# The first block of the first FFN: both token halves on the first half of the inputs, partial sums kept in SBUF, then the second half of the inputs

## Chip, cores and metric

The kernel runs on one core of a Trainium2 chip. The metric is device time in microseconds (us) of one execution, the median of the runs shown. The engines are TensorE (PE; its weight loads are PEld), VectorE (DVE), ScalarE (ACT), GpSimd (POOL) and SyncE (SP), which issues most of the DMAs.

## What is computed

One step of a hybrid decoder layer over 1024 prompt tokens and 32 sample tokens. The change lies at the very start, in the first of two SwiGLU FFNs (D_MODEL 1024, D_FF 2816):

```python
def swiglu(h, w_gate, w_up, w_down):
    return (jax.nn.silu(h @ w_gate) * (h @ w_up)) @ w_down

def modulated(h, g, i):
    return rms_norm(h, g) * (1 + scale[:, i]) + shift[:, i]

mod = (jax.nn.silu(c) @ p['w_ada'] + p['b_ada'])
x = x + 0.5 * gate[:, 0] * swiglu(modulated(x, p['g_ffn1'], 0), p['w1_gate'], p['w1_up'], p['w1_down'])
...
```

Attention, a gated MLP mixer and a second FFN of the same shape follow; the change does not touch them.

## The kernel before, in words

**Arithmetic.** Inputs are fp32. Each operand is split into a rounded part `hi` and a remainder `lo`, both fp32r, and `mm3` (L324, L325, L326) makes one product of three matmuls: hi·hi, hi·lo, lo·hi. A `hi` is a cast on ACT (L186 and L330 for weights, L741 for inputs), a `lo` a subtraction on DVE (L187, L331, L745).

**Blocks.** D_FF is cut into 11 blocks of 256. In each block, inputs (1024 in 2 halves of 512, each of 4 tiles j) and tokens (1024 in 2 halves of 512) make a 2 by 2 problem for the gate weights ("g") and the up weights ("u"). Blocks 1 to 10 do it in seven products instead of eight, on sums of weights (`sums_s` on POOL, L256 to L259) and on sums T1 to T4 of the inputs. Block 0 does it plainly in four stages, since the sums of the inputs don't exist yet. A stage is named (token half, input half). Its inputs are B11 for (0,0), B21 for (0,1), B12 for (1,0) and B22 for (1,1). In a stage each of g and u has two groups f of 12 matmuls, so a stage has 48. A group accumulates in one PSUM bank `psa`; there are four.

**Order before.** Block 0 runs (0,0), (0,1), (1,0), (1,1). A bank filled in (0,0) stays open and (0,1) adds to it; then `fin` empties it: for g a silu on ACT from PSUM (L862), for u a multiply on DVE with the silu (L864). The other branch of `fin`, used in later blocks, first adds a kept partial sum u: for g a DVE add (L860) and a silu from SBUF (L862), for u a DVE add into `hf` (L867) and a multiply on POOL (L868).

**Work between.** Fillers are generators whose steps are put into the program after every six matmuls (`tick`), at a pace given when they are added. The instructions of every engine then run in the order in which they were recorded; an engine stops at an instruction that waits. `mid1` adds and finishes the fillers at the stage bounds:
- `second` and `f1a`: norm and transposes of token half 1 (L525, L531, L553), giving B12 (ACT L755 and L741, DVE L745).
- ahead of (0,1), in one piece: the conditioning of quarters 2 and 3 of the inputs: `ada_q` (PE L362, ACT L365), `ada_m` (PE L374, DVE L377 to L379), `x_mod` (DVE L387, ACT L741, DVE L745), giving B21.
- `f1b`: the rest of the transposes, giving B22; then T1, T2 and T3 (`T23`), T4. One step of T1 or T2 is a subtraction on DVE (L775), a cast on ACT (L741), and the `lo` on DVE (L745). The subtractions of T3 and T4 are on POOL (L775); their casts and `lo`s are as the others.
- `s_norm` and `sample_gu`: the sample tokens (PE L404, L593, L610, L622, L628; DVE L407, L602, L603, L612, L642, L630, L650).

Block 1 begins with matmuls on the weights `ws`, whose `lo` (DVE L331) stands on DVE behind all of T1 to T4.

## Time and profile before

| | |
|---|---|
| median of 3 runs | 2425.75 us (2423.23 to 2427.13) |
| the profiled execution | 2428.47 us, span 2426.5 us |
| busy share of the span: PE, DVE, POOL, ACT | 96%, 56%, 36%, 34% |
| block 0, from its first matmul to the first one of block 1 | 29.43 to 108.22 us |

The profile is one execution. PE is busy almost throughout, but less so at the start: the first two of the 40 slices of the span show 6 and 8 tenths for PE, most others 9. So the stretch from 29 to 110 us is read by itself, stage by stage, with the work of each engine in order of time and what ended each idle stretch. A busy matmul runs into the next one: a group's pitch is the distance of starts, not the duration that a row names.

### The profile page before, as it was taken

How to read it: one execution, taken by the hardware profiler on the slowest of the kernel's cores; microseconds unless marked ns; L12 is line 12 of the kernel's file. 1: busy time of each engine (PE TensorE's matmuls, PEld its weight loads, DVE VectorE, ACT ScalarE, POOL GpSimd, SP SyncE). 2: the span in 40 equal slices, each digit the busy share in tenths (PEclk: the TensorE clock that was granted, in tenths of full speed). 3: DMA queues.
4: the chain of work that ended last, by engine and by line, in shares of the span. 5: the costliest groups of instructions: out<-in, count | busy, mean ns of one | idle time of the engine just before them, and what ended most of it. 6: DMA issues, size and time to landing. Idle time of an engine off the chain costs nothing.

```text
span 2426.5 us, 37080 instructions
## 1 busy us (share of the span) xinstructions
PE 2328.4 (96%) x12977; PEld 1738.7 (72%) x12977; DVE 1363.3 (56%) x1922; ACT 823.2 (34%) x1413; POOL 869.0 (36%) x822
## 2 busy tenths in 40 slices
PE   6899999999998999999999999999799999999998
PEld 4677777776776775556677767776577777777876
DVE  4756566564457555664443454445566565656557
ACT  4322222323234244543332242233332223233433
POOL 1455656550024123243323220011156565552125
PEclk8999999999999999999999999999899999999999
DMA  6243444459755237567877634443144434357743
GB/s 260 83 152 127 157 143 141 150 189 403 281 199 199 89 97 214 166 178 235 234 197 229 217 118 132 163 139 109 49 158 145 147 131 158 133 173 300 254 157 136
DMA packets 192784, 421.13 MB, mean 174 GB/s; under 512 B 22003, under 2 KB 80308, under 8 KB 192598
## 3 DMA queue, kind: packets, MB, share of 16 engines
q1 hardware_dynamic: 179510, 382.06, 46.7%
q0 software_dynamic: 12800, 36.19, 5.5%
q8 instruction: 102, 1.67, 0.3%
q14 instruction: 84, 0.69, 0.1%
q10 hardware_dynamic: 288, 0.52, 0.1%
HBM read 338.36 MB, written 78.23 MB: 172 GB/s over the span
## 4 chain that ended last, share of the span: by engine, by line
PE 78%; issue 5%; DVE 5%; DMA 5%; ACT 2%; POOL 2%; POOLq 1%; SPq 1%; DVEq 0%; ACTq 0%
PE psa L324 16%; PE psa L325 15%; PE psa L326 15%; PE psb L324 7%; PE psb L325 7%; PE psb L326 7%; PE pss L622 2%; DVE wlo L187 2%; PE psa L441 1%; PE pss L1587 1%; POOLq L1544 1%; DMA pk<-in_kvp 1%; PE pss L683 1%; DMA nat<-in_kvn 1%; PE pss L1633 1%
## 5 line engine op out<-in xcount | busy, mean ns | idle before, releaser
L187 DVE TENSOR_TENSOR wlo<-w,whi 128x1024 fp32r<-128x1024 f32 (+1 forms) x273 | 306.0, 1163 | 177.6 <-ACT whi L186 177.1
L324 PE MATMUL psa<-xT,ws 128*128 128x512 f32 x800 | 317.7, 397 | 0.0
L326 PE MATMUL psa<-xT,ws 128*128 128x512 f32 x800 | 311.9, 390 | 2.0 <-DVE ws L331 2.0
L325 PE MATMUL psa<-xT,ws 128*128 128x512 f32 x800 | 312.4, 391 | 0.0
L186 ACT CAST whi<-w 128x1024 fp32r<-128x1024 f32 (+1 forms) x273 | 241.2, 927 | 138.6 <-PE psb L325 35.9
L324 PEld LDWEIGHTS psa<-xT,ws 128*128 128x128 f32 x800 | 150.1, 188 | 45.7 <-ACT h L862 8.2
L326 PEld LDWEIGHTS psa<-xT,ws 128*128 128x128 f32 x800 | 150.2, 188 | 34.9 <-DVE ws L331 2.8
L325 PEld LDWEIGHTS psa<-xT,ws 128*128 128x128 f32 x800 | 150.2, 188 | 29.5
L868 POOL TENSOR_TENSOR h<-hf,h 128x512 f32<-128x512 f32 x60 | 93.1, 1552 | 218.0 <-DVE hf L867 180.9
L331 DVE TENSOR_TENSOR ws<-wsum,ws 128x512 fp32r<-128x512 f32 x160 | 153.0, 956 | 24.1 <-ACT ws L330 24.1
L324 PE MATMUL psa<-xT,whi 128*128 128x512 f32 x384 | 161.7, 421 | 1.6 <-ACT xT L741 1.6
L325 PE MATMUL psa<-xT,whi 128*128 128x512 f32 x384 | 153.6, 400 | 0.0
L326 PE MATMUL psa<-xT,wlo 128*128 128x512 f32 x384 | 153.0, 399 | 0.0
L331 DVE TENSOR_TENSOR ws<-w,ws 128x512 fp32r<-128x512 f32 x120 | 120.0, 1000 | 50.5 <-ACT ws L330 50.5
L324 PE MATMUL psa<-whi 128*128 128x512 f32 x308 | 124.9, 405 | 6.3 <-ACT whi L186 6.3
L325 PE MATMUL psa<-wlo,whi 128*128 128x512 f32 x308 | 121.8, 396 | 7.5 <-DVE wlo L187 7.5
L324 PE MATMUL psb<-xT,ws 128*128 128x512 f32 x320 | 127.1, 397 | 0.0
L325 PE MATMUL psb<-xT,ws 128*128 128x512 f32 x320 | 125.1, 391 | 0.0
L324 PE MATMUL psb<-whi 128*128 128x512 f32 x308 | 124.8, 405 | 0.0
L326 PE MATMUL psb<-xT,ws 128*128 128x512 f32 x320 | 124.6, 389 | 0.0
L326 PE MATMUL psa<-whi,wlo 128*128 128x512 f32 x308 | 121.4, 394 | 0.0
L1545 POOL DMA_DIRECT2D nat<-in_kvn x128 | 70.9, 554 | 140.4 <-issue 54.1
(397 smaller groups left out, 4898.4 us busy)
## 6 DMA issues: line engine op xcount, KB each, us to landing
wada<-in_w_ada SPq DMA_DIRECT2D x72, 512.0 KB, 7.1
x<-x SPq DMA_DIRECT2D x40, 512.0 KB, 5.6
pk<-in_kvp SPq DMA_DIRECT2D x128, 144.0 KB, 3.4
pk<-in_kvp POOLq DMA_DIRECT2D x128, 144.0 KB, 3.6
w<-w1h SPq DMA_DIRECT2D x35, 512.0 KB, 6.8
w<-w2h SPq DMA_DIRECT2D x35, 512.0 KB, 7.0
nat<-in_kvn SPq DMA_DIRECT2D x128, 128.0 KB, 2.9
nat<-in_kvn POOLq DMA_DIRECT2D x128, 128.0 KB, 3.0
```

The source lines that it names most:

```text
L186: self.nc.scalar.copy(hv(w.hi), src)
L187: self.nc.vector.tensor_tensor(out=hv(w.lo), in0=src, in1=hv(w.hi), op=ALU.subtract)
L324: nc.tensor.matmul(out, sh, mh, start=first, stop=False, skip_group_check=cont)
L325: nc.tensor.matmul(out, sh, ml, start=False, stop=False, skip_group_check=cont)
L326: nc.tensor.matmul(out, sl, mh, start=False, stop=last, skip_group_check=cont)
L331: self.nc.vector.tensor_tensor(out=lo, in0=src, in1=hi, op=ALU.subtract)
L441: nc.tensor.matmul(ps[32 * k:32 * k + 32, 256 * qq:256 * qq + 256], self.sc[:, 4 * kh + k, :], t[:, k, :], start=(kh == 0), stop=(kh == 1))
L622: self.nc.tensor.matmul(ps[32 * j:32 * j + 32, cols], st[:, k, :], mv, start=(k < 4), stop=(k >= nk - 4))
L683: self.nc.tensor.matmul(ps[32 * j:32 * j + 32, 0:256], hT[:, f, :], r[f][:, j // 2, c], start=(f == 0), stop=(f == 1))
L868: nc.gpsimd.tensor_tensor(out=g, in0=t, in1=g, op=ALU.mult)
L1544: v = eng.value_load(self.pt[0:1, 32 * b + i:32 * b + i + 1], min_val=0, max_val=self.a[name].shape[0] - 1)
L1545: eng.dma_start(out=out, in_=self.a[name][bass.ds(v, 1)].rearrange(pat))
```

## The change

`plan_ffn` gets a switch, on for the first FFN and off for the second. With it block 0 runs (0,0), (1,0), (0,1), (1,1). Each of the eight groups of the first two stages is closed and copied by ACT from PSUM to SBUF (`uv`); the groups of the last two stages open a new bank, and `fin` gets the copy as its u. In `mid1` the conditioning of quarters 2 and 3 becomes a filler in (1,0), f1b, T1 and `s_norm` stay in (0,1), and T2, T3, T4 and `sample_gu` share (1,1).

```diff
+        plan["conv"] = ((0, 0, "g"), (1, 0, "u"), (0, 1, "g")) if turns else ((0, 0, "g"), (0, 0, "u"), (0, 1, "g"))
+        plan["order"] = [(0, 0), (1, 0), (0, 1), (1, 1)] if turns else [(0, 0), (0, 1), (1, 0), (1, 1)]
...
-                for half in range(2):
-                    for kh in range(2):
+                for i, (half, kh) in enumerate(plan["order"]):
...
-                                if not kh:
+                                held = (half, f, n) in part
+                                if not kh or held:
                                     T[n, f] = self.psa()
...
                                 if kh:
-                                    fin(n, "%d%d" % (f + 1, half + 1), None, T[n, f])
+                                    fin(n, "%d%d" % (f + 1, half + 1), part.get((half, f, n)), T[n, f])
+                                elif plan["turns"]:
+                                    if not f:
+                                        uv = self.u([P, 2, 512], F32, name="uv")
+                                    part[half, f, n] = uv[:, f]
+                                    nc.scalar.copy(uv[:, f], T[n, f])
...
-        plan1 = k.plan_ffn("w1")
+        plan1 = k.plan_ffn("w1", True)
-        plan2 = k.plan_ffn("w2")
+        plan2 = k.plan_ffn("w2", False)
...
             if stage == (0, 0):
                 k.f1 = k.add(second(), 1.6)
+            elif stage == (1, 0):
+                k.f1.finish()
+
+                def quarters():
+                    for q in (2, 3):
+                        k.ada_q(q, k.psb)
+                        yield
+                    for q in (2, 3):
+                        k.ada_m(q)
+                    for q in (2, 3):
+                        k.x_mod(X1, f01, q)
+                        yield
+
+                k.f1 = k.add(quarters(), 1.5, 4.5)
             elif stage == (0, 1):
                 k.f1.finish()
-                for q in (2, 3):
-                    k.ada_q(q, k.psb)
-                for q in (2, 3):
-                    k.ada_m(q)
-                for q in (2, 3):
-                    k.x_mod(X1, f01, q)
                 k.f1 = k.add(chain(f1b, T1), 1.1)
                 k.f2 = k.add(k.s_norm(0, k.ada_rows()), 0.95)
-            elif stage == (1, 0):
-                k.f1.finish()
-                k.f2.finish()
-                k.f1 = k.add(T23, 1.2)
-                k.f2 = k.add(sample_gu(plan1["b"][0]), 1.2)
             elif stage == (1, 1):
                 k.f1.finish()
                 k.f2.finish()
-                k.f1 = k.add(T4, 1.3)
+                k.f1 = k.add(chain(T23, T4), 0.85)
+                k.f2 = k.add(sample_gu(plan1["b"][0]), 1.2)
             elif stage == (2, 0):
                 k.f1.finish()
+                k.f2.finish()
```

The lines of `mm3` and behind it stand three lower in the changed kernel (L326 is L329 there, L331 is L334, L642 is L645, L745 is L748, L775 is L778, L860 is L863, L862 is L865, L867 is L870, L868 is L871). The order in which instructions stand shows at three places what moves; `hf` is the sum of a kept and a new partial sum, `xt` is T2, `wsum` the weight sums of block 1.

PE, from the end of the second stage's matmuls or from within them. Before, the end of (0,0), the conditioning, the start of (0,1):

```order
L326 MATMUL psa<-xT,wlo 128x512
L362 MATMUL psb<-wada,sc 32x256 x32
L374 MATMUL pss<-cst,g_196 128x1 x8
L324 MATMUL psa<-xT,whi 128x512
L325 MATMUL psa<-xT,whi 128x512
```

Changed, within (1,0), from the second `ada_q` on:

```order
L365 MATMUL psb<-wada,sc 32x256 x16
L327 MATMUL psa<-xT,whi 128x512
L328 MATMUL psa<-xT,whi 128x512
L329 MATMUL psa<-xT,wlo 128x512
L327 MATMUL psa<-xT,whi 128x512
L328 MATMUL psa<-xT,whi 128x512
L329 MATMUL psa<-xT,wlo 128x512
L377 MATMUL pss<-cst,g_196 128x1 x8
```

The conditioning has moved behind 30 to 42 matmuls of (1,0), and six more follow it before (0,1) begins.

DVE, from the second step of T1 to the first copy of the sample's G. Before:

```order
L775 TENSOR_TENSOR xf<-xf 128x512
L745 TENSOR_TENSOR xT<-xf,xT 128x512
L864 TENSOR_TENSOR h<-h,psa 128x512
L775 TENSOR_TENSOR xf<-xf 128x512
L745 TENSOR_TENSOR xT<-xf,xT 128x512
L612 COPY xsT<-pss 128x2x4x32
L775 TENSOR_TENSOR xf<-xf 128x512
L745 TENSOR_TENSOR xT<-xf,xT 128x512
L864 TENSOR_TENSOR h<-h,psa 128x512
L775 TENSOR_TENSOR xt<-xf 128x512
L745 TENSOR_TENSOR xT<-xt,xT 128x512
L642 COPY G<-pss 128x256
```

Changed:

```order
L778 TENSOR_TENSOR xf<-xf 128x512
L748 TENSOR_TENSOR xT<-xf,xT 128x512
L870 TENSOR_TENSOR hf<-uv,psa 128x512
L778 TENSOR_TENSOR xf<-xf 128x512
L748 TENSOR_TENSOR xT<-xf,xT 128x512
L615 COPY xsT<-pss 128x2x4x32
L778 TENSOR_TENSOR xf<-xf 128x512
L748 TENSOR_TENSOR xT<-xf,xT 128x512
L870 TENSOR_TENSOR hf<-uv,psa 128x512
L778 TENSOR_TENSOR xt<-xf 128x512
L748 TENSOR_TENSOR xT<-xt,xT 128x512
L645 COPY G<-pss 128x256
```

The two multiplies have become adds into `hf`; the rest stands as before, and four adds for g (L863) stand elsewhere in this row of work.

POOL, from the sample's norm to the weight sums. Before:

```order
L519 TENSOR_TENSOR srs<-srs,mhalf 128x1
L775 TENSOR_TENSOR xf<-xf 128x512 x4
L775 TENSOR_TENSOR xf<-xf,xt 128x512 x4
L256 TENSOR_TENSOR wsum<-w 128x512
L257 TENSOR_TENSOR wsum<-wsum,w 128x512
L258 TENSOR_TENSOR wsum<-w 128x512
L259 TENSOR_TENSOR wsum<-w,wsum 128x512
```

Changed:

```order
L871 TENSOR_TENSOR h<-hf,h 128x512 x2
L778 TENSOR_TENSOR xf<-xf 128x512 x3
L259 TENSOR_TENSOR wsum<-w 128x512
L260 TENSOR_TENSOR wsum<-wsum,w 128x512
L261 TENSOR_TENSOR wsum<-w 128x512
L262 TENSOR_TENSOR wsum<-w,wsum 128x512
L778 TENSOR_TENSOR xf<-xf 128x512
L778 TENSOR_TENSOR xf<-xf,xt 128x512
L871 TENSOR_TENSOR h<-hf,h 128x512
L778 TENSOR_TENSOR xf<-xf,xt 128x512 x3
L871 TENSOR_TENSOR h<-hf,h 128x512
```

Four multiplies are new on POOL. Two stand ahead of T3's subtractions, the weight sums have moved ahead of T3's last one and of T4, and a multiply stands within T4.

## Rows read from the trace of the kernel before

**Rows 1.** The page's busy time, share and instructions of each engine over the whole span.

```profile
PE 2328.4 (96%) x12977; PEld 1738.7 (72%) x12977; DVE 1363.3 (56%) x1922; ACT 823.2 (34%) x1413; POOL 869.0 (36%) x822
```

**Rows 2.** Busy time of each engine in five stretches: (0,0); the conditioning; to the first step of T1; to block 1's first `lo` matmul; block 1 from there. Columns: stretch, its length, busy time and instructions by engine, granted TensorE clock, DMA share, GB/s.

```profile
29.40:50.70 21.30, 17.73 (x69) 12.99 (x69) 11.57 (x19) 12.79 (x21) 4.50 (x8) 0.81 0.56 223
50.70:58.40 7.70, 5.67 (x82) 3.92 (x81) 1.73 (x9) 1.87 (x4) 0.00 (x0) 0.96 0.18 53
58.40:73.00 14.60, 14.05 (x67) 10.41 (x68) 8.65 (x15) 9.42 (x16) 0.55 (x1) 0.79 0.00 1
73.00:109.80 36.80, 29.63 (x153) 22.16 (x151) 29.94 (x38) 12.21 (x22) 17.04 (x12) 1.00 0.31 100
109.80:160.00 50.20, 50.16 (x254) 39.25 (x254) 31.53 (x41) 13.09 (x24) 27.60 (x19) 1.00 0.40 135
```

**Rows 3.** PE in order of time: start, duration, line, operation, and in brackets the idle time before it and what ended it.

```profile
40.58 0.39 PE L553 MATMUL psb<-cst,xs 128*128 128x128 f32 x1 [1.14 <-DVE xs L531]
...
41.19 0.63 PE L325 MATMUL psa<-xT,whi 128*128 128x512 f32 x1
41.62 0.63 PE L326 MATMUL psa<-xT,wlo 128*128 128x512 f32 x1
...
44.40 0.40 PE L325 MATMUL psa<-xT,whi 128*128 128x512 f32 x1
44.63 0.40 PE L326 MATMUL psa<-xT,wlo 128*128 128x512 f32 x1
...
50.68 3.66 PE L362 MATMUL psb<-wada,sc 128*32 128x256 f32 x64
54.27 1.05 PE L374 MATMUL pss<-cst,g 128*128 128x1 f32 x8
55.73 1.02 PE L374 MATMUL pss<-cst,g 128*128 128x1 f32 x8 [0.41 <-DVE mod L378]
58.37 0.80 PE L324 MATMUL psa<-xT,whi 128*128 128x512 f32 x1 [1.62 <-ACT xT L741]
...
64.39 0.51 PE L326 MATMUL psa<-xT,wlo 128*128 128x512 f32 x1
...
109.84 0.50 PE L326 MATMUL psa<-xT,ws 128*128 128x512 f32 x1 [1.00 <-DVE ws L331]
```

**Rows 4.** The chain of work that ended last, 73 to 110 us: start, duration, what.

```profile
73.05 0.70 DVE xf L775
73.77 0.63 ACT xT L741
...
92.36 0.35 DVE G L642
92.75 0.66 PE pss L628 x4
...
109.10 0.69 DVE ws L331
```

**Rows 5.** DVE in order of time, columns as in rows 3.

```profile
73.05 0.68 DVE L775 TENSOR_TENSOR xf<-xf 128x512 f32<-128x512 f32 x1
74.42 1.28 DVE L745 TENSOR_TENSOR xT<-xf,xT 128x512 fp32r<-128x512 f32 x1 [0.69 <-ACT xT L741]
...
85.11 0.67 DVE L864 TENSOR_TENSOR h<-h,psa 128x512 f32<-128x512 f32 x1
85.71 0.68 DVE L775 TENSOR_TENSOR xt<-xf 128x512 f32<-128x512 f32 x1
...
97.26 0.69 DVE L775 TENSOR_TENSOR xt<-xf 128x512 f32<-128x512 f32 x1
...
99.79 7.50 DVE L745 TENSOR_TENSOR xT<-xf,xT 128x512 fp32r<-128x512 f32 x5
...
124.58 0.69 DVE L860 TENSOR_TENSOR h<-uv,psa 128x512 f32<-128x512 f32 x1 [0.34 <-PE psa L326]
```

**Rows 6.** DVE's groups of 40 to 73 us (the one row with 688) and of 73 to 109.8 us: count, busy time, mean ns of one, idle time before them and what ended it.

```profile
L745 DVE TENSOR_TENSOR xT<-xf,xT 128x512 fp32r<-128x512 f32 x12 | 8.0, 688 | 6.6 <-ACT xT L741 6.6
...
L745 DVE TENSOR_TENSOR xT<-xf,xT 128x512 fp32r<-128x512 f32 x13 | 15.4, 1206 | 4.2 <-ACT xT L741 4.2
L745 DVE TENSOR_TENSOR xT<-xt,xT 128x512 fp32r<-128x512 f32 x4 | 4.8, 1204 | 2.9 <-ACT xT L741 2.9
L864 DVE TENSOR_TENSOR h<-h,psa 128x512 f32<-128x512 f32 x4 | 2.7, 676 | 0.6 <-PE psa L326 0.6
```

**Rows 7.** POOL in order of time, columns as in rows 3.

```profile
73.86 1.29 POOL L775 TENSOR_TENSOR xf<-xf 128x512 f32<-128x512 f32 x1 [1.99 <-ACT h L862]
...
99.27 1.75 POOL L256 TENSOR_TENSOR wsum<-w 128x512 f32<-128x512 f32 x1
...
123.65 1.75 POOL L666 TENSOR_TENSOR wt<-wd 128x512 f32<-128x512 f32 x1
```

**Rows 8.** ACT in order of time, columns as in rows 3.

```profile
73.77 0.62 ACT L741 CAST xT<-xf 128x512 fp32r<-128x512 f32 x1 [0.86 <-DVE xf L775]
...
112.44 0.59 ACT L853 COPY uv<-psa 128x512 f32<-128x512 f32 x1 [5.10 <-PE psa L326]
```

**Rows 9.** Issues of SP: two loads of block 1's gate weights in order of time, and the time from issue to landing of such loads (last number).

```profile
89.40 0.80 SPq L163 DMA_DIRECT2D w<-in_w1g  x2
...
w<-in_w1g SPq DMA_DIRECT2D x6, 512.0 KB, 4.4
```

More of the change, by code (lines that the diff above doesn't have):

```diff
@@ L210, in unit_b, with plan_ffn @@
         return self.unit([r], [(r, ident, ident)], shape, fold)
-    def plan_ffn(self, pre):
+    def plan_ffn(self, pre, turns):
         a = self.a
@@ L245, in plan_ffn @@
         plan["pre"] = pre
+        plan["turns"] = turns
+        plan["conv"] = ((0, 0, "g"), (1, 0, "u"), (0, 1, "g")) if turns else ((0, 0, "g"), (0, 0, "u"), (0, 1, "g"))
+        plan["order"] = [(0, 0), (1, 0), (0, 1), (1, 1)] if turns else [(0, 0), (0, 1), (1, 0), (1, 1)]
         return plan
@@ L912, in ffn @@
                 ht, h = new_h(), hA
-                T = {}
-                for half in range(2):
-                    for kh in range(2):
+                T, part = {}, {}
+                for i, (half, kh) in enumerate(plan["order"]):
                         mid((half, kh))
@@ L923, in ffn @@
                                     self.sums_s(plan["b"][1]["rg"], plan["b"][1]["s"]["g"])
-                            hi, lo = self.use(e[n, kh], (n, kh) != ("u", 1) and not half, 0)
+                            hi, lo = self.use(e[n, kh], (half, kh, n) in plan["conv"], 0)
                             for f in range(2):
-                                if not kh:
+                                held = (half, f, n) in part
+                                if not kh or held:
                                     T[n, f] = self.psa()
@@ L929, in ffn @@
                                 for j in range(4):
-                                    self.mm3(T[n, f], (hi[:, j, c], lo[:, j, c]), (x[j][:, 0], x[j][:, 1]), not kh and j == 0,
-                                             kh == 1 and j == 3)
+                                    self.mm3(T[n, f], (hi[:, j, c], lo[:, j, c]), (x[j][:, 0], x[j][:, 1]), (not kh or held) and j == 0,
+                                             (kh == 1 or plan["turns"]) and j == 3)
                                     if j % 2:
```

## The prediction

> **What bounds the kernel now.** I read the page's busy shares first, then a table of stretches, then PE's order of time, then the chain that ended last and each engine behind it. Over the span PE is the bound, busy 96% [rows 1]. By stretch this holds from block 1 on: from 109.8 us PE is busy 50.16 of 50.20 us, at the full clock [rows 2]. Whatever delays the start of block 1 is therefore not caught up: it moves the end by as much. Ahead of that PE loses time. In the conditioning it is busy 5.67 of 7.70 us, and the next matmuls run at half clock (1.2 of 2.4 GHz): the pitch is 0.43 us (41.19 to 41.62) after one idle stretch, 0.23 us (44.40 to 44.63) once the clock is back; after the conditioning the low clock lasts from 58.37 to about 64.4 [rows 3], the stretch's mean is 0.79 [rows 2]. These are the losses that a fuller PE in that place could win back.
>
> But from 73 to 109.8 us another engine leads. DVE is busy 29.94 of 36.80 us [rows 2], and the chain that ended last runs DVE, ACT, DVE from 73.05 on; PE's own pieces in it wait for DVE's copies (L628 at 92.75 behind L642), and block 1's first `lo` matmul at 109.84 waits for DVE's L331 at 109.10 [rows 3, 4]. What DVE does there is T1 to T4, and DVE reaches L331 only when these are behind it.
>
> Why that takes so long: a `lo` (L745) takes 688 ns up to 73 us and 1206 ns behind it [rows 6]. At 74.42 it takes 1.28 us and POOL's subtraction runs from 73.86 to 75.15; the five at 99.79 take 7.50 us while POOL makes weight sums, the first in 1.75 us; yet the add at 124.58, with one operand in PSUM, takes 0.69 us beside POOL's L666 [rows 5, 7]. So here a DVE operation on two SBUF operands waits until POOL's running operation ends, and one on a PSUM operand doesn't.
>
> **Part by part.** All times are of the profiled execution (2428.47 us, span 2426.5); a difference is carried over to the median, 2425.75.
>
> *The eight copies.* 8 x 0.59 = 4.7 us on ACT [rows 8], which is busy 12.79 of 21.30 and 1.87 of 7.70 us there [rows 2]. A bank is needed 48 matmuls after its group ended, 48 x 0.23 = 11 us; that hides them. Without this cover each would cost PE 0.59. I take 0, except one ahead of a weight cast, below.
>
> *The conditioning moves into (1,0).* (1,0) starts at 50.7, where (0,0) ends. 30 matmuls (6.9), half of L362 (1.83), 6 (1.4), the other half (1.83), 6 (1.4): L374 starts at 64.0, not at 54.27. Behind it come 0.41 of wait and 2.1 of L374, then six matmuls, so that only some 0.2 us of the old 1.62 wait stays ahead of (0,1) at 68.1 [rows 3]. The clock there: PE has run matmuls until 62, so I take it as full; at half clock up to 3 us more.
>
> *When T1 starts.* From L374 to T1's first subtraction it was 73.05 - 54.27 = 18.8 us [rows 3, 5]. The steps between are the same. The full clock saves up to (64.4 - 58.4)/2 = 3 us of PE there. But B21's `lo`s come as late after L374 as before, so the first twelve matmuls of (0,1) can't run ahead of them; the copy in front of the weight cast delays L187 by 0.6; and two adds for g (L863, as L860 is called in the changed kernel) enter DVE. Net I take 17.8: T1 starts at 64.0 + 17.8 = 81.8. Bounds: 79.0 (all 3 us and more of it saved) and 82.8 (nothing).
>
> So T1 starts 81.8 - 73.05 = 8.75 us later. PE has by then done 48 matmuls more (11 us), but T1 to T4 don't need PE.
>
> *T1 to the first of T2* took 85.71 - 73.05 = 12.66 us [rows 5]. Each of the four `lo`s was held by POOL's T3 subtraction for some 0.6 us (1.28 against 0.688 [rows 5, 6]). These subtractions now stand behind two new multiplies, so POOL is silent until the first `hf`, and of the four only one `lo` is held: 12.66 - 3 x 0.6 = 10.8. A gain of 1.9; bounds 10.3 (none held) and 12.7.
>
> *T2 and T3 of tiles 0 to 2* took 97.26 - 85.71 = 11.55 us. POOL had then done T3 long before. Now it starts, at the second `hf`, ten operations one behind the other: multiply, T3 0 to 2, four weight sums, T3 3, T4 0. A DVE operation on SBUF operands gets in between two of them, at their pitch of about 1.7 us (99.27: 1.75 when held in turn; 73.86: 1.29 alone [rows 7]): T2 0 `lo`, T3 0 `lo` (which now also waits for its own subtraction), T2 1, its `lo`, T3 1 `lo`, T2 2, its `lo`, T3 2 `lo`. Ten operations, 16.6 us, from 10.85 to 27.4 behind T1's start; DVE ends at 28. The add and silu of g (L863, L865) sit on that path but fit into a hold. So 17.2: a loss of 5.65. Bounds: 9.3 if nothing is ever held, and 20. (Unheld, a step of T2 is 1.37 from subtraction to `lo`, 73.05 to 74.42, and 0.6 to the next start, as from 85.11 to 85.71 [rows 5]: three of 1.97, three `lo`s of 0.6, and 1.6 for a copy, an add and a silu.)
>
> *The rest, to L331,* took 109.10 - 97.26 = 11.84 us. Now: G copy 0.34, L863 0.61, T2 and T3 of tile 3 with a silu in the way (3.1), the sample (1.5), T4 0 (0.95): to 34.4 with the add L870. Then POOL's multiply (1.3) stands ahead of T4 1 to 3, each 1.3 on POOL with cast and `lo` behind, the `lo` of one held by the subtraction of the next: 7.1, and 0.6 for the last add. Together 14.2: a loss of 2.4. Bounds 8.4 and 16.
>
> The multiply that L864 did at 676 ns [rows 6] has become an add of the same length, so its change on DVE is nothing; the price is POOL's. The Trainium skill (Perfetto Trace Analysis, Optimizing Scalar/DVE Operations) warns that moving work from DVE to GpSimd might not help since both share an SBUF read port. By this rule the sum is the one above; without it, by the lower bounds, it is the rival of no change, below.
>
> *Clock at block 1.* PE stands idle for some 12 us behind the second sample product (L631 waits for G's second copy, 28.3) and some 5 ahead of block 1's first `lo`. After a like stretch (transposes one by one, each behind 1.14 us of idle, the last at 40.58) the half clock lasted until shortly ahead of 44.40 [rows 3], which cost half of 3.5 us, 1.7. The first idle stretch falls inside the wait for DVE and costs nothing; the second costs 1.7. Bounds 0 and 3.
>
> *SP.* The weights of block 1 that POOL sums are issued at 89.40 behind L622 and land 4.4 us later [rows 9]. If they wait for the same product in the new place, at about 96, they land at 100.8, 19 behind T1's start, which would delay the sums by two to three us within the held stretch; taken as 0, inside the upper bound.
>
> **Sum.** +8.75 (T1 later) - 1.9 + 5.65 + 2.4 (T1 to L331) + 1.7 (clock) = +16.6 us. PE's own gain (fuller around 51 to 70) is in the first term: it ends in a longer wait. 2425.75 + 16.6 = 2442.
>
> **Rivals.**
>
> *PE leads, faster.* From 58.4 to 109.8 PE is busy 14.05 + 29.63 us [rows 2]; 48 matmuls of it (11) now lie ahead and some 3 us were half clock: 29.7 are left, and with 1.6 of stops at (0,1) they end at 68.1 + 31.3 = 99.4 in place of 109.8: -10.4, 2415. It decides if DVE's chain ends by 99; but even unheld (10.3 + 9.3 + 8.4 = 28 us) it ends at 109.8. The Trainium skill (Perfetto Trace Analysis, Optimization Strategy) says that a kernel with several regimes may gain by interleaving them; this rival is what that would give here. Against it stands 29.94 of 36.80 [rows 2]: work is pushed into the regime that DVE leads. Chance 0.06.
>
> *No change.* POOL runs in the gaps of DVE, and L331 stands at 81.8 + 28 = 109.8: +0.7, with the clock up to +3: 2426 to 2429. For it: 0.69 us of wait in every step is room for half a POOL operation. Against: 1206 ns with 12 POOL operations in that stretch [rows 2, 6], where there are now 16. Chance 0.09.
>
> *Half of it.* Holds as large as before (36.05 from T1 to L331): +8.75 + 0 to 1.7: 2434 to 2436. Chance 0.2, counted to the forecast's side.
>
> *More.* The late loads and a low clock through (1,1) and the start of block 1: 2448 and above. Chance 0.1.
>
> *It does not do what it says:* a copy holds a bank and PE stops in (1,0). ACT's order has each copy tens of matmuls ahead of its need. It would end slower, by 0.59 a copy; 0.01.
>
> **How the numbers follow.** Forecast 0.54, half 0.2, more 0.1, the copies 0.01: slower 0.85. A measurement of this kernel can tell about 0.2% (4.9 us) from none: same 0.09, faster 0.06. The range leaves out the two small rivals and the end of "more": 2431 to 2449.
>
> **What would show it.** Right: PE without its 1.62 stop at (0,1) and few half-clock matmuls around 60 to 70; T1's first subtraction (L778) near 82; `lo`s (L748) near 0.69 us for two T1 tiles and near 1.7 behind; long PE waits for L645 and L615; the first L329 of block 1 on `ws` near 124 instead of 109.84, and block 1 on at PE's pace. Wrong: that matmul before 110, or `lo`s of 0.7 us beside POOL's run of ten operations, or PE stops in block 1 that shrink.

## The result, and the profile after

The changed kernel takes 2442.57 us (2440.64 to 2449.55) beside 2426.44 us (2423.23 to 2427.55) of the kernel before on the same chip: ratio 1.0072, 95% interval 1.0057 to 1.0087, slower by about 16 us. The execution that was profiled is the slowest of them, 2449.55 us with a span of 2446.8; the other spans were 2439.0 to 2441.7. Its trace is therefore read for where block 0 loses time, and single times in it may be late by 1 to 3 us: the second L377 starts at 67.52 here, and at 64.09 to 67.31 in e1, e5, e7, e8 and e9 below, which have the same code up to there.

Stretches, columns as in rows 2: (1,0) with the conditioning; (0,1) to T1; T1 to the start of block 1; block 1.

```profile
50.70:68.00 17.30, 16.89 (x128) 12.42 (x126) 2.30 (x5) 5.48 (x9) 0.00 (x0) 1.00 0.09 25
68.00:82.00 14.00, 12.34 (x72) 8.68 (x73) 10.27 (x21) 9.11 (x16) 0.23 (x1) 1.00 0.23 71
82.00:126.00 44.00, 23.79 (x113) 16.81 (x112) 30.88 (x41) 13.91 (x25) 24.43 (x17) 0.80 0.20 62
126.00:176.00 50.00, 50.00 (x249) 39.08 (x249) 30.75 (x41) 13.09 (x24) 26.77 (x19) 0.97 0.39 128
```

The change does for PE what it says: around the conditioning PE is busy 16.89 of 17.30 us at the full clock, where it was 5.67 of 7.70 and then a granted clock of 0.79 [rows 2]. All of it and more is lost in the third of these stretches, where PE is busy 23.79 of 44.00 us; DVE is busy 30.88 and POOL 24.43, against 17.04 of 36.80 for POOL [rows 2]. Block 1 runs at PE's pace again.

PE in order of time, columns as in rows 3:

```profile
66.16 0.95 PE L377 MATMUL pss<-cst,g 128*128 128x1 f32 x8
67.52 1.02 PE L377 MATMUL pss<-cst,g 128*128 128x1 f32 x8 [0.41 <-DVE mod L381]
70.89 0.50 PE L328 MATMUL psa<-xT,whi 128*128 128x512 f32 x1 [0.23 <-DVE xT L748]
...
111.04 1.11 PE L631 MATMUL pss<-cst,G 128*128 128x128 f32 x4 [11.41 <-DVE G L645]
...
123.68 0.80 PE L327 MATMUL psa<-xT,ws 128*128 128x512 f32 x1 [5.86 <-ACT ws L333]
...
125.08 0.79 PE L329 MATMUL psa<-xT,ws 128*128 128x512 f32 x1 [0.18 <-DVE ws L334]
...
129.05 0.40 PE L329 MATMUL psa<-xT,ws 128*128 128x512 f32 x1
```

and block 1's twelfth matmul before:

```profile
112.01 0.39 PE L326 MATMUL psa<-xT,ws 128*128 128x512 f32 x1
```

The stop of 1.62 us ahead of (0,1) is 0.23 now. Two long waits have come: 11.41 us for the copy of G, and 5.86 for the first weight sum. Block 1's first `lo` matmul starts at 125.08 in place of 109.84 [rows 3], and its twelfth matmul at 129.05 in place of 112.01. The second difference, 17.04, is the larger by 1.80, the half clock of the matmuls in between.

DVE, from T1's first subtraction to the first weight sum:

```profile
83.48 0.69 DVE L778 TENSOR_TENSOR xf<-xf 128x512 f32<-128x512 f32 x1
...
90.26 0.99 DVE L748 TENSOR_TENSOR xT<-xf,xT 128x512 fp32r<-128x512 f32 x1 [0.68 <-ACT xT L744]
...
94.08 0.69 DVE L778 TENSOR_TENSOR xt<-xf 128x512 f32<-128x512 f32 x1
...
98.28 1.11 DVE L748 TENSOR_TENSOR xT<-xf,xT 128x512 fp32r<-128x512 f32 x1 [1.49 <-ACT xT L744]
99.31 1.75 DVE L778 TENSOR_TENSOR xt<-xf 128x512 f32<-128x512 f32 x1
...
108.90 1.75 DVE L748 TENSOR_TENSOR xT<-xf,xT 128x512 fp32r<-128x512 f32 x1
110.57 0.41 DVE L645 COPY G<-pss 128x256 f32<-128x256 f32 x1
...
116.25 0.68 DVE L870 TENSOR_TENSOR hf<-uv,psa 128x512 f32<-128x512 f32 x1
120.25 3.58 DVE L748 TENSOR_TENSOR xT<-xf,xT 128x512 fp32r<-128x512 f32 x3 [3.32 <-ACT xT L744]
...
124.34 0.69 DVE L334 TENSOR_TENSOR ws<-w,ws 128x512 fp32r<-128x512 f32 x1
```

T1 starts at 83.48 (73.05 before [rows 5]), T2 at 94.08, and L334 comes at 124.34 (109.10 before [rows 4]).

POOL beside it:

```profile
94.31 1.60 POOL L871 TENSOR_TENSOR h<-hf,h 128x512 f32<-128x512 f32 x1 [3.60 <-DVE hf L870]
95.86 4.65 POOL L778 TENSOR_TENSOR xf<-xf 128x512 f32<-128x512 f32 x3
100.48 1.71 POOL L259 TENSOR_TENSOR wsum<-w 128x512 f32<-128x512 f32 x1
...
108.39 1.70 POOL L778 TENSOR_TENSOR xf<-xf,xt 128x512 f32<-128x512 f32 x1
117.08 1.27 POOL L871 TENSOR_TENSOR h<-hf,h 128x512 f32<-128x512 f32 x1 [6.98 <-DVE hf L870]
118.31 4.15 POOL L778 TENSOR_TENSOR xf<-xf,xt 128x512 f32<-128x512 f32 x3
```

From 94.31 to 110.09 POOL runs ten operations without a gap. Then it stands idle 6.98 us ahead of the third multiply, until DVE's `hf` at 116.25 is there, and the last three subtractions of T4 stand behind that multiply. They need nothing of it; DVE waits 3.32 us for them, and PE 5.86.

DVE's groups of 82 to 126 us, columns as in rows 6:

```profile
L748 DVE TENSOR_TENSOR xT<-xf,xT 128x512 fp32r<-128x512 f32 x13 | 12.4, 954 | 9.9 <-ACT xT L744 9.6
```

A `lo` takes 954 ns, less than the 1206 before [rows 6], but 9.9 us are spent waiting ahead of them where it was 4.2. DVE isn't held longer by POOL's running operations; it waits more for what POOL delivers late.

### The profile page after: what moved, and what is told of

Read it like the earlier page. It is cut to its first block, busy times and chain, and to the rows that moved or that the text cites. A ratio compares the mean times of both kernels' runs of the same rounds, so it can differ in the third digit from the quotient of the medians.

```text
span 2446.8 us, 37093 instructions
## 1 busy us (share of the span) xinstructions
PE 2330.5 (95%) x12977; PEld 1737.0 (71%) x12977; DVE 1365.2 (56%) x1926; ACT 827.8 (34%) x1421; POOL 875.4 (36%) x826
## 4 chain that ended last, share of the span: by engine, by line
PE 75%; issue 6%; DMA 5%; DVE 5%; ACT 3%; POOL 3%; POOLq 2%; SPq 1%; DVEq 0%; ACTq 0%
PE psa L327 16%; PE psa L328 15%; PE psa L329 15%; PE psb L327 7%; PE psb L328 6%; PE psb L329 6%; PE pss L625 2%; DVE wlo L187 1%; DMA wada<-in_w_ada 1%; POOLq L1552 1%; PE psa L444 1%; PE pss L1595 1%; DMA nat<-in_kvn 1%; PE pss L686 1%; DMA pk<-in_kvp 1%
## 5 line engine op out<-in xcount | busy, mean ns | idle before, releaser
L187 DVE TENSOR_TENSOR wlo<-w,whi 128x1024 fp32r<-128x1024 f32 (+1 forms) x273 | 306.0, 1163 | 184.1 <-ACT whi L186 177.4
L329 PE MATMUL psa<-xT,ws 128*128 128x512 f32 x800 | 312.6, 391 | 1.2 <-DVE ws L334 1.2
L871 POOL TENSOR_TENSOR h<-hf,h 128x512 f32<-128x512 f32 x64 | 99.2, 1549 | 237.5 <-DVE hf L870 193.7
L329 PEld LDWEIGHTS psa<-xT,ws 128*128 128x128 f32 x800 | 150.7, 188 | 34.6 <-DVE ws L334 2.3
L334 DVE TENSOR_TENSOR ws<-wsum,ws 128x512 fp32r<-128x512 f32 x160 | 155.4, 971 | 24.4 <-ACT ws L333 24.4
L329 PE MATMUL psa<-xT,wlo 128*128 128x512 f32 x384 | 152.4, 397 | 0.0
L334 DVE TENSOR_TENSOR ws<-w,ws 128x512 fp32r<-128x512 f32 x120 | 118.7, 989 | 50.5 <-ACT ws L333 50.5
L329 PE MATMUL psb<-xT,ws 128*128 128x512 f32 x320 | 124.6, 389 | 0.0
L329 PE MATMUL psa<-whi,wlo 128*128 128x512 f32 x308 | 121.1, 393 | 0.0
L329 PE MATMUL psb<-whi,wlo 128*128 128x512 f32 x308 | 120.9, 392 | 0.0
```

What stands on the lines that cost most here:

```text
L187: self.nc.vector.tensor_tensor(out=hv(w.lo), in0=src, in1=hv(w.hi), op=ALU.subtract)
L329: nc.tensor.matmul(out, sl, mh, start=False, stop=last, skip_group_check=cont)
L334: self.nc.vector.tensor_tensor(out=lo, in0=src, in1=hi, op=ALU.subtract)
L871: nc.gpsimd.tensor_tensor(out=g, in0=t, in1=g, op=ALU.mult)
```

## The experiments

Two measures stand beside each other. The time and its ratio are those of the whole kernel. The twelfth matmul of block 1 tells what happened in block 0 alone: from it to the end the same code took 2308.8 to 2317.8 us in the traces of all kernels but the last, so that scatter behind block 0 hides a few us in the time. "T1 to 12th" is the stretch from T1's first subtraction to that matmul. Each kernel left one trace; where nothing between T1 and the wait ahead of block 1 differs, the stretch repeats well (45.57 in the changed kernel, 45.71 in e7, 43.88 in e9 with its 1.8 us of clock). The ratios are to runs of the kernel before beside each group of kernels, whose medians were 2423.79 to 2426.44, so kernels of different groups are better compared by ratio than by median.

| kernel | median us | ratio to before, 95% | T1 starts | 12th | T1 to 12th |
|---|---|---|---|---|---|
| before | 2426.44 | | 73.05 | 112.01 | 38.96 |
| after | 2442.57 | 1.0072 (1.0057 to 1.0087) | 83.48 | 129.05 | 45.57 |
| e1, multiplies left out | 2433.18 | 1.0031 (1.0017 to 1.0044) | 82.47 | 121.16 | 38.69 |
| e2, T1 in (1,0) | 2435.92 | 1.0035 (1.0025 to 1.0045) | 51.52 | 122.22 | |
| e3, copies, adds and multiplies in the old order | 2431.14 | 1.0019 (1.0008 to 1.0030) | 73.48 | 116.23 | 42.75 |
| e4, T1 to T4 early | 2432.20 | 1.0025 (1.0015 to 1.0035) | 50.13 | 118.76 | |
| e5, multiplies on DVE | 2441.76 | 1.0064 (1.0043 to 1.0085) | 81.76 | 124.40 | 42.64 |
| e6, e4 and multiplies on DVE | 2431.75 | 1.0026 (1.0017 to 1.0036) | 50.10 | 118.94 | |
| e7, 16 added matmuls | 2440.43 | 1.0060 (1.0041 to 1.0080) | 82.02 | 127.73 | 45.71 |
| e8, weight sums late | 2441.24 | 1.0071 (1.0051 to 1.0092) | 80.03 | 122.90 | 42.87 |
| e9, 26 added matmuls | 2441.63 | 1.0076 (1.0059 to 1.0093) | 81.95 | 125.83 | 43.88 |
| e10, old placing, new order | 2436.11 | 1.0056 (1.0039 to 1.0072) | 74.53 | 122.31 | 47.78 |
| e11, e10 and multiplies on DVE | 2435.62 | 1.0053 (1.0036 to 1.0070) | 73.12 | 120.21 | 47.09 |
| e12, e4 and the sample slower | 2437.59 | 1.0054 (1.0040 to 1.0068) | 50.77 | 116.95 | |

The theory to test: the price is (a) the later start of T1 to T4, and (b) the partial sums' four multiplies in POOL's queue. Rivals: the adds and copies themselves; the new order of the products; the granted clock.

### e1: the four multiplies left out

```diff
                     nc.vector.tensor_tensor(out=t, in0=u, in1=ps, op=ALU.add)
-                    nc.gpsimd.tensor_tensor(out=g, in0=t, in1=g, op=ALU.mult)
+                    if b:
+                        nc.gpsimd.tensor_tensor(out=g, in0=t, in1=g, op=ALU.mult)
```

> The changed kernel without the four GpSimd multiplies of gate and up in block 0 (L871; block 1 keeps its own). What is left out: those products, so half of the hidden values of block 0 that enter the output are the up parts alone. Theory (GpSimd's ten operations of T2 to T4 run beside, and behind, the multiplies, and VectorE stands behind GpSimd): with the multiplies gone GpSimd reaches its operations of T2 to T4 some 3 to 5 us earlier and block 1 starts that much earlier: 2.0 to 5 us less than the changed kernel, about 2438 to 2440. Rival 1 (TensorE's own queue sets the start of block 1, or GpSimd's multiplies fall into VectorE's gaps): within 1 us of the changed kernel. Rival 2 (the partial-sum adds on VectorE are the price, not GpSimd): within 1 us as well, since the adds stay.

Measured: 2433.18, ratio 1.0031; the interval lies wholly below that of the changed kernel. The gain is larger than expected, 7.9 us at the twelfth matmul and 9 to 10 in time. T1 to 12th falls from 45.57 to 38.69, to what it was before the change (38.96). Both rivals are out. T1 still starts 9.4 us late. So the two parts of the price separate: the late start is what is left (1.0031), and all that T1 to T4 take longer goes with the multiplies. Of these 6.9 us, 5.1 lie between T1 and L334 (35.79 in place of 40.86; 36.05 before), and 1.8 behind it: in e1 the matmuls from block 1's first `lo` to the twelfth take 2.16 us, as before, where the changed kernel's half clock makes 3.97 of them. Why more than expected: the last subtractions of T4 no longer stand behind an operation that waits for `hf`:

```profile
101.32 3.38 POOL L778 TENSOR_TENSOR xf<-xf,xt 128x512 f32<-128x512 f32 x2
106.75 1.27 POOL L778 TENSOR_TENSOR xf<-xf,xt 128x512 f32<-128x512 f32 x1 [2.05 <-DVE xt L778]
110.78 1.29 POOL L778 TENSOR_TENSOR xf<-xf,xt 128x512 f32<-128x512 f32 x1 [2.76 <-DVE xt L778]
```

The last one starts at 110.78; in the changed kernel the three began at 118.31.

### e2: T1 one stage earlier

```diff
                 k.f1 = k.add(quarters(), 1.5, 4.5)
+                k.f2 = k.add(T1, 1.3)
             elif stage == (0, 1):
                 k.f1.finish()
-                k.f1 = k.add(chain(f1b, T1), 1.1)
+                k.f2.finish()
+                k.f1 = k.add(f1b, 1.1)
```

> The changed kernel with only T1 moved, from behind f1b in stage (0,1) to stage (1,0), as a filler of its own beside the quarters. Nothing is left out. Theory (VectorE's chain T1 to T4 starts late and sets the start of block 1): VectorE is busy 2.3 of 17.3 us in stage (1,0), so T1's 10.6 us leave the chain, and T2 then starts when the second add of the half is done, at about 88 us in place of 94: 5 to 6.5 us less than the changed kernel, about 2436 to 2437.5. If T1 gets in the way of the quarters of the modulation in that stage, up to 3 us of this are lost. Rival (TensorE leads, or the add of the partial sums is the price): within 1 us of the changed kernel.

Measured: 2435.92, the twelfth matmul 6.8 us earlier. The theory's number; the rival is out. T1's first subtraction moves to 51.52, into the stage where DVE was busy 2.30 of 17.30 us, and T2 begins at 87.49 in place of 94.08. That the change records T1 behind f1b in the third stage costs it some two fifths of what it loses by the twelfth matmul, and about half by the ratios.

### e3: copies, adds and multiplies in the old order

The order of the stages and the fillers of the kernel before, with the partial sums copied to SBUF, added and multiplied as in the changed kernel:

```diff
-        plan["conv"] = ((0, 0, "g"), (1, 0, "u"), (0, 1, "g")) if turns else ((0, 0, "g"), (0, 0, "u"), (0, 1, "g"))
-        plan["order"] = [(0, 0), (1, 0), (0, 1), (1, 1)] if turns else [(0, 0), (0, 1), (1, 0), (1, 1)]
+        plan["conv"] = ((0, 0, "g"), (0, 0, "u"), (0, 1, "g")) if turns else ((0, 0, "g"), (0, 0, "u"), (0, 1, "g"))
+        plan["order"] = [(0, 0), (0, 1), (1, 0), (1, 1)] if turns else [(0, 0), (0, 1), (1, 0), (1, 1)]
...
```

> The kernel before (its order of the stages and its fillers) with the partial sums of the first half of the inputs brought to SBUF by ScalarE, added on VectorE and multiplied on GpSimd, as the changed kernel does; the order is not changed. Nothing is left out. Theory (the later start of the fillers is the price, evacuation is not): T1 keeps its place at 73 us, the multiplies of GpSimd cost T2 to T4 0 to 5 us, so 2426 to 2431, most likely 2428. Rival (the evacuation and the adds are the price): nearly the whole difference, some 12 to 16 us, 2438 to 2442.

Measured: 2431.14, at the upper end of the theory's range and far from the rival's 2438. T1 starts where it did (73.48), and the twelfth matmul comes 4.2 us late. So keeping the partial sums in SBUF is not free even with nothing moved, and not the main price either. e3 doesn't separate the copies from the adds and multiplies behind them; e1, where copies and adds stay and T1 to T4 take no longer than before, points at the multiplies.

### e4: T1 to T4 one stage earlier

T1 as in e2, and:

```diff
-                k.f1 = k.add(chain(f1b, T1), 1.1)
+                k.f1 = k.add(chain(f1b, T23), 0.83)
...
-                k.f1 = k.add(chain(T23, T4), 0.85)
+                k.f1 = k.add(T4, 1.3)
```

> The changed kernel with its fillers placed one stage earlier: T1 in stage (1,0), T2 and T3 behind f1b in stage (0,1), T4 and the sampling of the next block's weights in stage (1,1). Nothing is left out. Theory (the start of VectorE's chain is the whole price of the change, and the order itself costs TensorE nothing): the chain reaches its last weight sum at about 100 to 104 us, where TensorE is nearly out of other work (109 in the kernel before), so block 1 starts 5 to 10 us before that of the kernel before: 2416 to 2422, faster than the kernel before. Rival (the new order has a price of its own on TensorE or on the modulation of the second half of the tokens): no better than the kernel before, 2426 or more.

Measured: 2432.20, and the twelfth matmul at 118.76, 6.75 behind the kernel before. Better than the changed kernel by 10 us, but the expectation (faster than before) fell, and the rival holds: there is a price that an early start doesn't remove. The chain of waits of e4 shows where it is, T1 to T4 being early (start, duration, what):

```profile
97.05 0.61 DVE hf L870
98.10 0.92 issue
99.02 5.93 POOL xf L778 x4
...
106.64 1.74 DVE xT L748
108.38 0.35 DVE G L645
108.77 1.10 PE pss L631 x4
```

An `hf`, a multiply on POOL (it stands at 97.79), four subtractions behind it, a cast, a `lo`, the copy of G, PE. DVE is busy only 27.77 of the 43.56 us from 73.00 to 116.56. So this chain is set less by the load of one engine than by four queues, each in order. e4 without its multiplies was not run.

### e5 and e6: the multiplies on DVE

```diff
-                    nc.gpsimd.tensor_tensor(out=g, in0=t, in1=g, op=ALU.mult)
+                    (nc.gpsimd if b else nc.vector).tensor_tensor(out=g, in0=t, in1=g, op=ALU.mult)
```

e5 is the changed kernel with this edit, e6 is e4 with it.

> The changed kernel with block 0's four multiplies of gate and up (L871) on VectorE in place of GpSimd; placement unchanged, nothing left out. Theory (the price of the multiplies is their place in GpSimd's queue: the third stands there waiting for TensorE's last tile, 6.98 us idle, with three subtractions of T4 behind it): almost all of what leaving them out gave, less VectorE's own four operations of about 0.7 us, so 5 to 8 us under the changed kernel, 2434 to 2437. Rival (the multiplies cost what they take, on whichever engine, because VectorE is the bound): at most 2 us under the changed kernel, 2439 or more, since VectorE gets 2.8 us more to do.

> The kernel with T1, T2/T3 and T4 one stage earlier (e4), and the four multiplies on VectorE as well; nothing left out. Theory (what is left of e4's loss is GpSimd held by the multiplies: 4.77 and 4.21 us idle ahead of them while T2 to T4 stand behind, and with it the copy of the sample's G, which TensorE waits 3.6 us for, and the half clock after these waits): 3 to 5 us under e4, 2427 to 2430, about even with the kernel before. Rival (e4's loss is the sample's own chain of steps, which waits for VectorE whatever GpSimd does): within 1.5 us of e4, 2431 or more.

e5 measured 2441.76, where the theory said 2434 to 2437 and the rival 2439 or more. Its trace shows a gain, T1 to 12th 42.64 in place of 45.57: the stretch from the second copy of G to L334 is 10.62 us (110.01 to 120.63) instead of 13.77, since T4 no longer waits behind a multiply; but four operations more stand on DVE. Those 3 us can't be told from nothing by these times, whose intervals overlap almost wholly. Against e1 it splits the 5.1 us that the multiplies cost between T1 and L334 (40.86 with them on POOL, 38.87 on DVE, 35.79 without): about 2 are their place in POOL's queue, about 3 stay with them on DVE. The other 1.8 of the 6.9 are the clock, which e5 has in part. The theory, which gave nearly all of it to the queue, was wrong in that. e6 measured 2431.75, as e4: the rival holds there, and POOL's multiplies were not what kept e4 from its mark.

### e7 and e9: matmuls in the wait ahead of block 1

Added ahead of block 1's first product (16 in e7, 26 in e9), into the bank that this product then overwrites:

```diff
                 A[n] = self.psa()
+                if plan["turns"] and b == 1 and n == "g":
+                    for i in range(16):
+                        x = X["B11"][i % 4][:, 0]
+                        nc.tensor.matmul(A[n], x[:, 0:P], x, start=True, stop=True)
```

> The changed kernel with 16 matmuls of 128x512 whose result is overwritten, ahead of block 1's first product on TensorE (added work, nothing left out). They fill 3.6 us (at the pitch 0.227) of the 5.9 us in which TensorE waits there for T4 and the first weight sum. Theory (the half clock of block 1's first eleven matmuls, pitch 0.43, is a consequence of that wait and a part of the price): these matmuls run at the full pitch, and the twelfth starts 1 to 1.8 us earlier against the first: 2439 to 2440, 1 to 1.8 us under the changed kernel. Rival (the clock falls in the remaining 2.3 us, or the dummies come out of the way too late): 0 to 2 us above the changed kernel.

> The changed kernel with 26 matmuls of 128x512 whose result is overwritten ahead of block 1's first product (added work, nothing left out): at the pitch 0.227 they fill 5.9 us, all of the wait there, where 16 of them had left 2.9 us open, and the half clock had come back. Theory (that wait is what costs the clock, about 1.7 us): block 1's first twelve matmuls run at the full pitch, the twelfth starting about 2.7 us behind the first in place of 5.4, and the whole kernel takes 1 to 2 us less than the changed kernel. Rival (the half clock at block 1 comes from something else than this wait): the pitch stays 0.43 there, and the kernel is 0 to 1 us above the changed kernel.

PE in e7:

```profile
115.61 3.79 PE L856 MATMUL psa<-xT 128*128 128x512 f32 x16
122.31 0.50 PE L327 MATMUL psa<-xT,ws 128*128 128x512 f32 x1 [2.91 <-ACT ws L333]
...
123.72 0.79 PE L329 MATMUL psa<-xT,ws 128*128 128x512 f32 x1 [0.65 <-DVE ws L334]
```

and in e9:

```profile
115.94 6.05 PE L856 MATMUL psa<-xT 128*128 128x512 f32 x26
122.25 0.50 PE L327 MATMUL psa<-xT,ws 128*128 128x512 f32 x1 [0.25 <-ACT ws L333]
...
123.66 0.50 PE L329 MATMUL psa<-xT,ws 128*128 128x512 f32 x1 [0.67 <-DVE ws L334]
...
125.83 0.39 PE L329 MATMUL psa<-xT,ws 128*128 128x512 f32 x1
```

e7 leaves 2.91 us of wait, and the half clock comes back, as its rival had it: the twelfth matmul starts 127.73 - 122.31 = 5.42 us behind the first, as in the changed kernel (5.37). e9 leaves 0.25, and it is 3.58. So the wait costs 5.37 - 3.58 = 1.8 us of clock, what the theory said, in the trace. The kernels' times (2440.43, 2441.63) show neither this nor its absence; the expectation of 1 to 2 us less in time was not borne out by a measurement that can't resolve it.

### e8: the weight sums later

```diff
-                                else:
+                                elif not plan["turns"]:
                                     self.sums_s(plan["b"][1]["rg"], plan["b"][1]["s"]["g"])
```

> The changed kernel with the four weight sums on GpSimd (L259 to L262) recorded where block 1 first asks for them, behind all of T4, in place of between T2 and T3; nothing left out. Theory (GpSimd's queue paces T2 to T4): T3's last subtraction starts at 100.5 in place of 106.7 us, TensorE gets the copy of G some 6 us earlier, and block 1's first product starts some 6 us earlier; its second product then waits for the sums, which gives 1 to 3 us of it back: 3 to 5 us under the changed kernel, 2436 to 2438. Rival (GpSimd has 6.98 us idle behind the sums anyway, so that VectorE or TensorE sets the pace): within 1 us of the changed kernel, or above it by up to 3 us, since the sums then come late for block 1.

Measured 2441.24, as the rival has it; in the trace T1 to 12th is 42.87, 2.7 us less. POOL's T3 ends earlier (the second copy of G comes 24.3 us behind T1's start in place of 27.1), but the sums then begin at 119.93, and DVE waits 4.40 us for the first of them. So about 3 us of T2/T3's slowness are these four operations, and the move gives part of it back. By time nothing is shown.

### e10 and e11: the new order with the old placing

The conditioning at once at the second stage's start, f1b, T1 and the sample's norm in that stage, T2/T3 and the sample's products in the third, T4 in the fourth, as in the kernel before; order, copies, adds and multiplies as changed:

```diff
-                k.f1 = k.add(quarters(), 1.5, 4.5)
...
+                k.f1 = k.add(chain(f1b, T1), 1.1)
+                k.f2 = k.add(k.s_norm(0, k.ada_rows()), 0.95)
             elif stage == (0, 1):
...
-                k.f1 = k.add(chain(f1b, T1), 1.1)
-                k.f2 = k.add(k.s_norm(0, k.ada_rows()), 0.95)
+                k.f1 = k.add(T23, 1.2)
+                k.f2 = k.add(sample_gu(plan1["b"][0]), 1.2)
             elif stage == (1, 1):
...
-                k.f1 = k.add(chain(T23, T4), 0.85)
...
+                k.f1 = k.add(T4, 1.3)
```

> The changed kernel's order of the four stages, partial sums, copies and GpSimd multiplies, but the fillers by position as the kernel before has them: the quarters of the modulation at once at the second stage's start, f1b with T1 and the sample's norm beside them, T2/T3 and the sample's products in the third stage, T4 in the fourth. Nothing is left out. Theory (the price of the change is the later start of VectorE's chain and the multiplies in GpSimd's queue, and the order of the products itself costs nothing): as the kernel before's order with copies alone (e3), T1 at about 73 us, 2428 to 2432. Rival (the order of the products has a price of its own, as e4's 2432 with T1 to T4 early suggests): 2434 or more.

> The kernel of e10 with block 0's four multiplies on VectorE in place of GpSimd; nothing left out. Theory (the multiplies' own time is on the path, on VectorE as on GpSimd, since VectorE has nearly no slack from T1 to the end of T4; what moving them saved in e5, some 3 us of 45, came from GpSimd's queue, and here only two of them stand in T2 to T4's way): within 2 us of e10, so 2427 to 2431. Rival (GpSimd alone is the price of the multiplies): 3 to 4 us under e10 and level with the kernel before, 2425 to 2427.

e10 measured 2436.11 and a ratio of 1.0056: the rival. With T1 at 74.53, as early as ever, the twelfth matmul still comes 10.3 us late, against 4.2 in e3, which differs from it in the order of the two middle stages and what hangs on it. So with the fillers in these places the order has a price of its own, some 6 us: 1.0 by T1's start, 3.4 from T1 to L334 (42.61 in place of 39.17), and 1.6 behind it, where e10's first matmuls of block 1 run at half clock (5.15 us from the first to the twelfth, 3.56 in e3). POOL in e10:

```profile
99.31 1.61 POOL L871 TENSOR_TENSOR h<-hf,h 128x512 f32<-128x512 f32 x1 [16.69 <-DVE hf L870]
100.89 1.73 POOL L778 TENSOR_TENSOR xf<-xf 128x512 f32<-128x512 f32 x1
104.74 1.29 POOL L871 TENSOR_TENSOR h<-hf,h 128x512 f32<-128x512 f32 x1 [2.12 <-DVE hf L870]
105.99 5.89 POOL L778 TENSOR_TENSOR xf<-xf,xt 128x512 f32<-128x512 f32 x4
```

and in e3:

```profile
79.12 1.59 POOL L871 TENSOR_TENSOR h<-hf,h 128x512 f32<-128x512 f32 x1 [6.81 <-issue]
84.31 1.61 POOL L871 TENSOR_TENSOR h<-hf,h 128x512 f32<-128x512 f32 x1 [3.60 <-DVE hf L870]
85.88 6.33 POOL L778 TENSOR_TENSOR xf<-xf 128x512 f32<-128x512 f32 x4
```

In the old order the first token half is finished in the second stage, and its two multiplies are over before POOL begins T3. In the new order no half is finished before the third stage: with these places of the fillers all the adds, silus and multiplies of both halves fall among T2 to T4, and POOL waits 16.69 us for the first `hf` with a subtraction of T3 behind. e11, the same with DVE's multiplies, is 2435.62, within 2 us of e10 as its theory said (its range, built on e10's, was too low by 4 to 5 us, as that one). So POOL's wait is not the price by itself: in e11 no operation on POOL waits for an `hf`, and T1 to L334 still takes 42.69 us, with DVE busy 34.93 of them. Both kernels have two adds for g (1.3 us) and a `lo` of weights (L187, 1.2) on DVE in that stretch which e3 has ahead of T1; how much of the 3.4 us is their work and how much waiting was not separated.

### e12: the sample's steps further apart

e4 with the sample's norm at 1.3 in place of 0.95, and its products spread from the fourth stage into block 1:

```diff
-                k.f2 = k.add(k.s_norm(0, k.ada_rows()), 0.95)
+                k.f2 = k.add(k.s_norm(0, k.ada_rows()), 1.3)
...
-                k.f2 = k.add(sample_gu(plan1["b"][0]), 1.2)
+                k.f2 = k.add(sample_gu(plan1["b"][0]), 2.4, 6.0)
             elif stage == (2, 0):
                 k.f1.finish()
-                k.f2.finish()
```

with `self.f2.finish()` ahead of block 1's `s_wd`.

> The kernel with T1 to T4 one stage earlier (e4), and the sample's chain of steps given more room on TensorE: the norm's filler at 1.3 in place of 0.95, and the sample's products of block 0 spread over the fourth stage and the start of block 1 (finished ahead of block 1's sample sums) in place of all in the fourth stage; nothing left out. Theory (with T1 to T4 early, what is left of e4's loss is TensorE waiting in its queue for the steps of the sample's chain: 3.1 for u, 2.0 for xsT, 1.0 and 3.6 for G, and half clock behind these waits): 5 to 8 us under e4, 2424 to 2427, level with the kernel before or a little under it. Rival (VectorE or GpSimd sets the end of T4 anyway, and the waits come back at block 1's first weight sum): within 2 us of e4, 2430 or more.

Measured: 2437.59, slower than e4; the rival. PE's waits of 20 to 130 us (what waited for what: us in total, times, longest):

```profile
PE psa L327 <- ACT ws L333: 8.2, 1, 8.2
...
PE pss L686 <- issue: 2.4, 1, 2.4
```

The waits for the copies of xsT and G are gone and come back as 8.2 us ahead of block 1, which starts at 112.12 in place of 115.01, with 2.2 us of PE's work (L625 and L631) put off into it: PE's own waits were not what made e4 late. The deferred steps then hold up the sample's sums, L686, by 2.4 us, at 126.94 where e4 had 124.53. Which of DVE, ACT and POOL would have to be relieved to bring e4 to the kernel before isn't settled: the chain there passes all three. No version of the new order that was run beats the kernel before; the best are e6 and e4.

## Why the prediction held, step by step

The forecast was 2442 from a sum of +16.6; the result is 2442.57, +16.1, and the trace puts block 1's twelfth matmul 17.0 later. The likeliest case came true. That the sum comes so near is in part luck: in this trace T1 starts 1.7 us later than predicted, and the three terms behind it are together 1.3 shorter. Each term can be set against the trace:

- **T1 later, +8.75 to 81.8.** 83.48 in the profiled execution, +10.4; 80.03 to 82.47 in e1, e5, e7, e8 and e9, which have the same fillers to there, so +7.0 to +9.4. L377 starts at 66.16 in the profiled execution, predicted 64.0 (62.73 to 65.87 in the other five); the stretch from it to T1 is 17.3 us, predicted 17.8. That this start is a price by itself is shown by e2 (T1 early: 6.8 us back) and e1 (start late, the rest as before: 1.0031).
- **T1 to the first of T2, -1.9.** 83.48 to 94.08 is 10.60, predicted 10.8, before 12.66; one `lo` of four is held (0.99), as predicted. e1 turns it round: with the multiplies gone POOL's subtractions start at once, and the stretch is 13.2.
- **T2 and T3 of tiles 0 to 2, +5.65.** To the second copy of G 16.49, predicted 17.2. The ten operations on POOL are there, back to back, from 10.83 behind T1's start (predicted 10.85) to 26.6 (27.4), and they pace DVE as described: the operation that comes while one of them runs ends behind it (last section). What the text had wrong is how long each is held. It has the `lo`s near 1.7 us; most are 0.9 to 1.1, since they come when POOL's operation is partly done, and the rest of the time DVE waits for what POOL delivers late. e8 gives the four weight sums about 3 us of it.
- **The rest, +2.4.** 13.77, predicted 14.2. The multiply ahead of T4's last three subtractions is there, with 6.98 us of idle POOL ahead of it. e1 and e5 show it: this stretch shrinks when the multiply isn't in POOL's queue.
- **Clock, +1.7.** 1.80 by the two starts, 1.8 by e9. The term with the smallest error, and the only one that came from a like wait in the trace of before.
- **Copies, 0.** No wait of PE for a bank in (1,0) has appeared. (With four banks a bank is needed again 36 matmuls after its group ended, not 48: 8 us, which still covers the copies.) What e3 adds to the old order, 4.2 us, comes with the multiplies rather than the copies, as far as e1 shows. The prediction had charged the add nothing, since the multiply before took as long on DVE, and the multiply to POOL alone; e5 shows that on DVE it costs about 3 us too.
- **SP, 0.** The worry was misplaced: the two loads of block 1's weights are issued between 70.08 and 79.67, 10 to 19 us earlier than before [rows 9], not behind the sample's product:

```profile
70.08 9.59 SPq L163 DMA_DIRECT2D w<-in_w1g  x2
```

The rival in which PE leads is out: PE does arrive early and then waits 17.3 us in two pieces. No change and half fall by the interval; half's own assumption (T1 to L331 as long as before) is met by e1 alone. "More" falls too: the loads came early, and the half clock in (1,1) (a pitch of 0.43 us from 111.80 on) is over before PE's wait of 5.86 us, which is DVE's.

Set beside e3, the trace gives the 17.0 us a plainer split than the prediction's terms: 10.4 are T1's later start, 3.1 what T1 to L334 take longer in e3 too (39.17, 36.05 before), 1.7 what they take longer still in the changed kernel (40.86), and 1.8 the clock. From T1 to L334 the changed kernel has the same adds and multiplies as e3, only later: two of the eight adds stand ahead of T1, two within it, four behind. So the price of the order that e10 shows, with all eight behind T1, is not a part of this loss; it says that leaving the fillers at their old places would not have saved the change.

On the contention the trace bears out the reading of rows 5 and 7. The subtraction at 99.31 ends at 101.06, 0.55 us behind POOL's of T3 (95.86 + 4.65 = 100.51), and the `lo` at 108.90 ends at 110.65, 0.56 behind POOL's of T4 (108.39 + 1.70 = 110.09). In e5 a multiply on DVE with two SBUF operands took 1.32 us beside a weight sum on POOL, and 0.69 without one; the add ahead of it, with one operand in PSUM, 0.68 in both places. The Trainium skill (SBUF — State Buffer, Who interferes with whom) has it so: a DVE instruction with two SBUF inputs contends with a GpSimd instruction that reads SBUF, one with at most one SBUF input, outside the modes that use both ports, doesn't.

## What to carry to other kernels

A gap in the leading engine is worth filling only if the work moved there doesn't push other work into the stretch that another engine leads: ask of each stage which engine ends last, and what arrives there later. Partial sums held aside cost more than their copies: the multiplies that finish them stand in an in-order queue, where unrelated operations wait behind one that waits for its data, and on another engine they still take their time. Read the position of the first work behind the change in the trace beside the time; here it showed 2 to 3 us in single traces that the time could not.

## What the runs showed of the hardware

The granted clock need not have fallen when work begins again behind a wait. In e5 PE waited 2.97 us for a weight sum, until 121.37, and the clock came down only from 122.6 on. Columns as in rows 2:

```profile
117.70:122.40 4.70, 1.73 (x7) 1.13 (x8) 4.67 (x8) 0.95 (x2) 0.00 (x0) 1.00 0.67 216
122.60:125.60 3.00, 3.00 (x8) 2.32 (x7) 2.86 (x3) 0.54 (x2) 1.78 (x1) 0.50 0.00 0
126.00:128.00 2.00, 2.00 (x10) 1.61 (x10) 0.69 (x1) 0.69 (x2) 0.00 (x0) 1.00 1.02 379
```

The wait and the first four matmuls behind it stand at 1.00 (2.4 GHz), the next 3 us at 0.50 (1.2 GHz), though PE is busy in all of them, and then it is full again. In e4 a wait of 0.93 us at the same place left the pitch at 0.23.

DVE's operations with both operands in SBUF and POOL's wait for each other, and the later one waits for the end of the other. From 40 to 130 us of the fourteen traces, 195 such operations of 128x512 began on DVE while POOL ran one: 192 of them ended 0.54 to 0.55 us behind POOL's, so that 0.69 us alone became as much as 1.79. The other way round, 153 of POOL's began while such an operation was under way on DVE, and all ended 1.12 to 1.16 us behind DVE's: the multiply at 94.31, begun beside the subtraction of 94.08, took 1.60, the one at 117.08, begun beside none, 1.27. The 34 adds on DVE with an operand in PSUM that ran beside POOL's took 0.67 to 0.69.
